# A hybrid encoder step in fp32: which groups of the two SwiGLU parts run as plain products and which as block products

## The chip, the cores and the metric

The kernel runs on one core of a Trainium2 chip, as one launch. The core has TensorE (PE, with its weight loads PEld), VectorE (DVE), ScalarE (ACT), GpSimd (POOL) and SyncE (SP), which issues the DMAs here. The metric is device time of one execution in microseconds: the median of three runs of the kernel before is 2302.98 us (2301.21 to 2305.12). Beside it stands one profiled execution.

## The reference

One layer of a streaming encoder on 1024 prompt tokens and 32 sample tokens, width 1024, all in fp32. Three sub-layers follow each other: a SwiGLU of inner width 2816, a pair of attention mixers side by side, and a second SwiGLU. Each is normalised before and after, and modulated by a vector `c` (one for the prompt, one for the sample):

```python
mod = jax.nn.silu(c) @ w_mod + b_mod
sh1, sc1, g1, sh2, sc2, g2, sh3, sc3, g3 = jnp.split(mod, N_MOD, axis=-1)
h = adaln_in(x, gains[0], sh1, sc1)
x = x + FFN_RES * g1[:, None] * rmsnorm(swiglu(h, w1_gate, w1_up, w1_down), gains[1])
...  # mixers with sh2, sc2, g2
h = adaln_in(x, gains[4], sh3, sc3)
x = x + FFN_RES * g3[:, None] * rmsnorm(swiglu(h, w2_gate, w2_up, w2_down), gains[5])
```

`swiglu(h)` is `(silu(h @ w_gate) * (h @ w_up)) @ w_down`. `w_mod` is 1024 x 9216, 36 MB of the weights.

## The kernel before, in words

**Layout and precision.** Activations lie with the width on partitions and tokens along the free axis. The 1056 tokens form three blocks: block 0 and block 1 with 384 tokens each, block 2 with 288 (256 of the prompt, 32 of the sample). A product of fp32 accuracy is made of three matmuls: each operand is split into a rounded part and a rest (ACT casts the first, `pair_of`; DVE or POOL subtracts for the second), and high x high, high x low and low x high are added up in PSUM (`product`).

**Two SwiGLU parts.** `ffn` is called twice, with the keys `h1` (first sub-layer) and `h3` (last). The inner width 2816 is cut into 11 groups of 256. A group has three stages: gate, up (`Mat`, weights of 1024 x 256, cut into four pieces A11 to A22 of 512 x 128) and down (`Rows`, 256 rows of `w_down`). A list of rounds says which group is done for which blocks; a stage is one round's gate, up or down, and the down stage of a round is queued behind the gate stage of the next. Each stage loads, casts and splits its own weights; the loads of the next stage start beside the present one.

**Plain and block products.** `plain` does one block: for each half f of the group's 256 columns two products of 12 matmuls (four k-tiles of 128 times three). Two blocks of 384 tokens then cost eight products a stage. `strassen` treats the pair (block 0, block 1) as one 2 x 2 block matrix product and needs seven: weight sums S1 to S4 on POOL (`ws`), token sums T1 to T4 made once for a part by `combos` (`z`, `t`), and ten additions a group on DVE that put the results together (tiles `sl` and `ut` from `gu` and `ge`). Block 2 stays plain inside it.

**Rounds before.** First part (`h1`): group 0 plain for the blocks as their norms come, groups 1 to 7 by block products with block 2 beside, groups 8 to 10 by block products for blocks 0 and 1 and then for block 2 alone. Last part (`h3`): group 0 plain for blocks 0 and 1, group 1 by block products, then groups 0 and 1 for block 2, then groups 2 to 10 by block products with block 2 beside.

**Work beside.** Generators in a list (`side`) do the other work in pieces: norms (`between`), `combos`, the rest of the modulation (`mod_all`), and the bias rows of the mixers (`bias_rows`). `step(n)` draws n pieces from the first of the list; `need` draws until one is done. Only the first 2048 columns of the modulation are made by matmuls at the start. The other 7168 columns go 384 at a time through `mod_aside`: four loads of 384 KB (`wma`), multiplied and accumulated for the prompt on DVE (`macc`, L247 and L249) and for the sample on ACT and POOL (`wmn`, `macc`, L250 to L255), then summed over partitions by small matmuls (`pms`) and turned into coefficients (`modT`, `acoef`, `gcoef`). Its buffers come from a pool of five that the weight sums, token sums and squares share. `per_group` is called with the group number after a round's up stage, and for round 0, whose up stage is done inside its gate stage, after the gate stage; for group 0 of the first part it is `mod_rest`, which starts the modulation and the bias rows.

**Order.** A scheduler sets each engine's order when the program is built; an engine then works through its queue in that order, and SP's queue of loads too. PSUM has two double banks for the down products and the pairs of block products (`p2`), and three single ones (`p1`). `r`, `w`, `ux`, `g`, `s` are the buffer counts of raw weights, split weights, extra activations, gated products and temporaries in a part.

## Time and profile before

| What | Value |
|---|---|
| median of three runs | 2302.98 us |
| profiled execution | 2300.64 us |
| its span, first to last instruction | 2298.9 us |
| mean granted TensorE clock | 0.966 |
| PE busy | 2140.8 us, 93% |
| DVE busy | 1449.5 us, 63% |
| ACT busy | 939.0 us, 41% |
| POOL busy | 810.0 us, 35% |
| moved by DMA | 186.10 MB, mean 81 GB/s |

The profile names engines, lines and tiles: `L249 DVE ... macc<-wma,csil,macc` is the accumulation of line 249 that writes `macc` from the loaded weights. The first SwiGLU runs from 42 to 894 us, the mixers follow, and the second SwiGLU starts at 1481 us. A matmul's own time overlaps the next one's, so a stage's time is read from the number of matmuls and the busy time of the stretch, and not from the mean of one. An engine's idle time is given with what ended it; idle time of an engine that nothing waits for costs nothing.

### The profile page before, as it was taken

The numbers are of one execution on the slowest core, as the hardware profiler recorded it, in microseconds if no ns is written. First come the engines' busy times: TensorE is split into PE (matmuls) and PEld (weight loads), VectorE is DVE, ScalarE is ACT, GpSimd is POOL, SyncE is SP. The second block draws the span as 40 slices with busy tenths as digits, with TensorE's granted clock in tenths as the row PEclk, the third lists the DMA queues.
The fourth block names the chain that finished last, engine by engine and source line by source line (L and its number), as shares of the span: only waits on it lengthen the run. The fifth ranks groups of instructions, "written<-read, shape, count | busy, mean of one in ns | idle before, by whom it ended". The sixth has DMA issues, their size and how long they took to land.

```text
span 2298.9 us, 35045 instructions
## 1 busy us (share of the span) xinstructions
PE 2140.8 (93%) x13644; PEld 2023.3 (88%) x13644; DVE 1449.5 (63%) x2722; ACT 939.0 (41%) x1990; POOL 810.0 (35%) x742
## 2 busy tenths in 40 slices
PE   7899999999999998999999899958999999999998
PEld 4888998999889997989888578858999999999997
DVE  5858667767775587667644775675644454444548
ACT  4454333433333344467644674434432223232225
POOL 2366555645554312200100322335133323332321
PEclk8999999999999998999999899979999999999999
DMA  8133323322342254110201211322311111111123
GB/s 322 59 94 113 92 78 92 117 80 89 95 129 72 65 187 144 54 48 25 66 14 39 80 37 47 134 61 66 111 56 56 46 46 56 56 38 54 38 65 115
DMA packets 150841, 186.10 MB, mean 81 GB/s; under 512 B 7980, under 2 KB 134356, under 8 KB 149524
## 3 DMA queue, kind: packets, MB, share of 16 engines
q1 hardware_dynamic: 150676, 183.87, 25.8%
q8 instruction: 107, 1.75, 0.3%
q14 instruction: 58, 0.48, 0.1%
HBM read 164.12 MB, written 22.86 MB: 81 GB/s over the span
## 4 chain that ended last, share of the span: by engine, by line
PE 54%; DVE 7%; POOL 4%; DMA 3%; ACT 2%; issue 2%; DVEq 0%; SPq 0%; POOLq 0%; ACTq 0%
PE gu L605 6%; PE ge L605 6%; PE dn L804 4%; PE dn L803 4%; PE dn L805 4%; PE g L605 4%; PE po L989 3%; POOL ws L570 2%; PE S L1028 2%; PE pq L349 2%; PE pq L351 2%; PE pq L350 2%; PE gate L605 2%; DMA raw<-in_w_up_dram 2%; PE pp L1052 1%
## 5 line engine op out<-in xcount | busy, mean ns | idle before, releaser
L547 DVE TENSOR_TENSOR w<-raw,w 128x512 fp32r<-128x512 f32 x298 | 257.2, 871 | 237.6 <-ACT w L546 229.2
L547 POOL TENSOR_TENSOR w<-ws,w 128x512 fp32r<-128x512 f32 x160 | 220.9, 1390 | 426.7 <-ACT w L546 426.7
L803 PE MATMUL dn<-gg,w 128*128 128x384 f32 (+1 forms) x1008 | 332.3, 330 | 16.8 <-DVE facc L810 10.7
L546 ACT ACTIVATE w<-raw 128x512 fp32r<-128x512 f32 x298 | 183.8, 627 | 370.1 <-PE gu L605 133.6
L804 PE MATMUL dn<-gg,w 128*128 128x384 f32 (+1 forms) x1008 | 326.6, 324 | 0.3 <-DVE gg L706 0.3
L805 PE MATMUL dn<-gg,w 128*128 128x384 f32 (+1 forms) x1008 | 326.1, 324 | 0.0
L810 DVE TENSOR_TENSOR facc<-dn,facc 128x768 f32<-128x768 f32 (+1 forms) x240 | 212.9, 887 | 179.6 <-PE dn L805 178.1
L605 PE MATMUL gu<-t,w 128*128 128x384 f32 x1440 | 265.4, 336 | 5.8 <-ACT w L546 3.6
L605 PEld LDWEIGHTS gu<-t,w 128*128 128x128 f32 x1440 | 249.1, 188 | 7.4 <-ACT w L546 3.9
L605 PE MATMUL g<-h_hi,w 128*128 128x288 f32 x1024 | 222.8, 295 | 1.5 <-DVE facc L810 1.5
L803 PEld LDWEIGHTS dn<-gg,w 128*128 128x128 f32 x1008 | 190.8, 189 | 24.4 <-DVE facc L810 14.9
L804 PEld LDWEIGHTS dn<-gg,w 128*128 128x128 f32 x1008 | 190.8, 189 | 0.6 <-DVE gg L706 0.6
L805 PEld LDWEIGHTS dn<-gg,w 128*128 128x128 f32 x1008 | 190.5, 189 | 0.0
L570 POOL TENSOR_TENSOR ws<-raw 128x512 f32<-128x512 f32 x80 | 118.5, 1482 | 194.9 <-DMA raw<-in_w_gate_dram 95.9
L605 PE MATMUL ge<-h,w 128*128 128x384 f32 x960 | 184.0, 335 | 0.1
L605 PEld LDWEIGHTS g<-h_hi,w 128*128 128x128 f32 x1024 | 172.0, 189 | 1.7 <-DVE facc L810 1.7
L546 ACT ACTIVATE w<-ws 128x512 fp32r<-128x512 f32 x160 | 98.6, 628 | 174.7 <-PE g L605 78.4
L605 PEld LDWEIGHTS ge<-h,w 128*128 128x128 f32 x960 | 166.4, 188 | 1.1 <-DVE w L547 0.7
L605 PE MATMUL g<-h_lo,w 128*128 128x288 f32 x512 | 151.4, 296 | 0.0
L249 DVE SCALAR_TENSOR_TENSOR macc<-wma,csil,macc 128x384 f32<-128x384 f32 (+1 forms) x133 | 123.6, 929 | 30.5 <-DMA wma<-in_w_mod_dram 29.0
L250 ACT ACTIVATE wmn<-wma,csil 128x384 f32<-128x384 f32 (+1 forms) x152 | 84.7, 602 | 117.7 <-DMA wma<-in_w_mod_dram 97.9
L605 PE MATMUL ge<-t,w 128*128 128x384 f32 x480 | 107.2, 362 | 23.1 <-ACT w L546 19.1
(298 smaller groups left out, 4625.5 us busy)
## 6 DMA issues: line engine op xcount, KB each, us to landing
raw<-in_w_gate_dram SPq DMA_DIRECT2D x54, 512.0 KB, 4.2
raw<-in_w_up_dram SPq DMA_DIRECT2D x54, 512.0 KB, 4.2
raw<-in_w_down_dram SPq DMA_DIRECT2D x54, 512.0 KB, 3.6
wma<-in_w_mod_dram SPq DMA_DIRECT2D x72, 384.0 KB, 3.3
raw<-in_w_in_dram SPq DMA_DIRECT2D x18, 512.0 KB, 4.5
raw<-in_w_out_dram SPq DMA_DIRECT2D x13, 512.0 KB, 4.3
wm<-in_w_mod_dram SPq DMA_DIRECT2D x8, 768.0 KB, 8.9
xr<-xs SPq DMA_DIRECT2D x16, 384.0 KB, 3.5
```

The source lines that it names most:

```text
L249: ve.scalar_tensor_tensor(acc[0], r[:, kk], csil[:, k, 0:1], acc[0], op0=OP.mult, op1=OP.add)
L250: ae.activation(n[:, kk], r[:, kk], AF.Copy, scale=csil[:, k, 1:2])
L349: te.matmul(ps, w[:, 0, k], hi, start=start, stop=False)
L546: ae.activation(w[:, 0], src, AF.Copy)
L547: (by or ve).tensor_tensor(w[:, 1], src, w[:, 0], op=OP.subtract)
L570: (ge if name in SUMS_POOL else ve).tensor_tensor(a[name], x, y, op=op)
L605: te.matmul(ps, w[a][:, k, :], x[b][k], start=first and k == 0 and q == 0, stop=last and k == n - 1 and q == 2, skip_group_check=True)
L803: te.matmul(ps[:, s, :w], h[:, k % 4, :], g[:, 0, :w], start=q == 0, stop=False)
L804: te.matmul(ps[:, s, :w], h[:, k % 4, :], g[:, 1, :w], start=False, stop=False)
L805: te.matmul(ps[:, s, :w], l[:, k % 4, :], g[:, 0, :w], start=False, stop=q == 1)
L810: ve.tensor_tensor(o, ps[:, :, :w], o, op=OP.add)
L989: te.matmul(po[64 * h:64 * h + 64, :n], vsl(j, h, kn), PT(h, j, kn), start=j == 0, stop=j == nt - 1)
```

## The change

It does five things.

- First part: groups 0 to 4 are plain (`PLAIN = 5`), groups 5 to 7 by block products with block 2 beside, groups 8 to 10 as before. `plain` takes several blocks of one stage, and draws five side pieces after every two products of a block, where round 0 drew ten and the block products one after each product; block products now draw two in both parts. `combos` is started at group 4's gate stage, ahead of all other side work, instead of at block 1 of round 0.
- Last part: groups 0 and 1 go plain for block 0, then for block 1, then for block 2 (`LEAD = 2`), and groups 2 to 10 by block products. Block 2's norm is started ahead of `combos`. The shared buffer `wu` for the first up stage is used in the first part alone.
- `combos` makes T3, T1 and T2 for both halves first and T4 last, and computes T4 from the finished T2.
- In rounds with one block, the low parts of A12, A22 and of the second half of the down weights are subtracted on POOL (`aside`, `shared`).
- The test ahead of `per_group` changes from "up stage, or gate stage of round 0" to "up stage, or round 0 of the first part", which holds for round 0's gate stage and for its down stage.

```diff
-ROUNDS = {"h1": (0, 3), "h3": (2, 0)}
+LEAD = 2
+LAST = 3
+PLAIN = 5
+STEPS = {"h1": (5, 5), "h3": (6, 6)}
...
-FFN2 = {"ux": 3, "r": 5, "w": 4, "g": 6, "s": 9}
+FFN2 = {"ux": 3, "r": 4, "w": 5, "g": 6, "s": 9}
...
+            self.aside = ("A12", "A22") if shared else ()
...
-                                          by=ge if name[0] == "S" else ve)
+                                          by=ge if name[0] == "S" or name in self.aside else ve)
...
-                self.w[q, hf] = pair_of(self.raw[q][:, 4 * hf:4 * hf + 4])
+                self.w[q, hf] = pair_of(self.raw[q][:, 4 * hf:4 * hf + 4], by=ge if self.shared and q else ve)
...
     def rounds(key):
...
+        both, n = (0, 1, 2), NF // 2
+        if key == "h3":
+            return [(g, (tb,)) for tb in both for g in range(LEAD)] + [(g, both) for g in range(LEAD, n)]
+        return [(g, both) for g in range(n - LAST)] + [(g, (0, 1)) for g in range(n - LAST, n)] + \
+            [(g, (2,)) for g in range(n - LAST, n)]
...
-        pace = PACE if key == "h1" else 2
+        pace = 2
+        fast = {r for r, (g, t) in enumerate(plan) if len(t) == 3 and (key == "h3" or g >= PLAIN) or len(t) == 2}
...
-            held = [stages.pop()] if r > 1 else []
+            held = [stages.pop()] if r else []
...
+                for tb in tbs:
+                    w = TB[tb][1]
                     ps = p1("gate" if what == "g" else "up")
...
+                    for d in range(2):
+                        product(ps[:, :w], w_[d], half(tb, d), d == 0, d == 1)
...
-                step((FAST if r == 0 else 3) if d else 2 * (r > 0))
+                    step(STEPS[key][len(tbs) > 1 or r == 0])
...
         if key == "h3":
+            begin((key, 2), between(F2[2], 2, 1, H3))
             begin((key, "T"), combos(H, T, tags))
-            begin((key, 2), between(F2[2], 2, 1, H3))
...
-                    if tb == 1 and key == "h1":
-                        begin((key, "T"), combos(H, T, tags))
...
+                if what == "g" and (key, gi) == ("h1", PLAIN - 1):
+                    begin((key, "T"), combos(H, T, tags), first=True)
+                plain(r, what, m, blocks, lambda n: nexts(n, 2 * len(blocks) - 1))
-            if what == "u" or r == 0 and what == "g":
+            if what == "u" or (key, r) == ("h1", 0):
                 if 2 in blocks:
                     per_group(gi)
```

The built program has 152 loads `wma` where it had 76. SP's queue just after the first part's x has been stored, before (`raw` are weights of a stage, `wma` the modulation's; x3 is three of the kind in a row):

```order
L586 DMA raw<-in_w_down_dram 128x1024 x2
L557 DMA raw<-in_w_gate_dram 128x4x256 x2
L557 DMA raw<-in_w_up_dram 128x4x256 x2
L241 DMA wma<-in_w_mod_dram 128x2x384 x7
L557 DMA raw<-in_w_gate_dram 128x4x256 x2
L241 DMA wma<-in_w_mod_dram 128x2x384 x3
```

and now:

```order
L244 DMA wma<-in_w_mod_dram 128x2x384 x9
L561 DMA raw<-in_w_gate_dram 128x4x256
L244 DMA wma<-in_w_mod_dram 128x2x384
L561 DMA raw<-in_w_gate_dram 128x4x256
L244 DMA wma<-in_w_mod_dram 128x2x384 x13
L590 DMA raw<-in_w_down_dram 128x1024 x2
L244 DMA wma<-in_w_mod_dram 128x2x384 x5
```

More modulation loads now stand between two loads of weights.

DVE's queue in group 2 of the first part, just ahead of the group's first accumulation of down products (`facc`), before:

```order
L249 SCALAR_TENSOR_TENSOR macc<-wma,csil,macc 128x384
L547 TENSOR_TENSOR w<-raw,w 128x512
L223 TENSOR_TENSOR modT<-modT,cst 128x2
L223 TENSOR_TENSOR modT<-modT,cst 128x2x2
L249 SCALAR_TENSOR_TENSOR macc<-wma,csil,macc 128x384
L227 SCALAR_TENSOR_TENSOR acoef<-modT,cst 128x2x2
L751 TENSOR_TENSOR sl<-gu,sl 128x384
L249 SCALAR_TENSOR_TENSOR macc<-wma,csil,macc 128x384 x2
L547 TENSOR_TENSOR w<-raw,w 128x512
L810 TENSOR_TENSOR facc<-dn,facc 128x768
```

and now:

```order
L252 SCALAR_TENSOR_TENSOR macc<-wma,csil,macc 128x384 x6
L250 TENSOR_SCALAR macc<-wma,csil 128x384
L252 SCALAR_TENSOR_TENSOR macc<-wma,csil,macc 128x384 x3
L267 COPY modT<-pms 128x2x3
L252 SCALAR_TENSOR_TENSOR macc<-wma,csil,macc 128x384
L226 TENSOR_TENSOR modT<-modT,cst 128x2x3
L252 SCALAR_TENSOR_TENSOR macc<-wma,csil,macc 128x384
L230 SCALAR_TENSOR_TENSOR acoef<-modT,cst 128x2x3
L550 TENSOR_TENSOR w<-raw,w 128x512
L252 SCALAR_TENSOR_TENSOR macc<-wma,csil,macc 128x384
L550 TENSOR_TENSOR w<-raw,w 128x512
```

Sixteen operations of the modulation (`macc`, `modT`, `acoef`) stand there now where seven stood, and the block additions (`sl<-gu`) are gone.

PE's queue at the start of the last part, from the second piece of the first gate stage on, before (`pr` spreads a norm's factor, `h` is the normalised block, `wu` the shared up weights):

```order
L605 MATMUL gate<-h,w 128x384 x13
L429 MATMUL pr<-ident,ry 128x128 x3
L605 MATMUL up<-h,wu 128x384 x4
L605 MATMUL gate<-h,w 128x384 x18
L605 MATMUL up<-h,wu 128x384 x32
L605 MATMUL up<-h,w 128x384 x12
```

and now:

```order
L609 MATMUL gate<-h,w 128x384 x13
L609 MATMUL up<-h,w 128x384 x22
L432 MATMUL pr<-ident,ry 128x128 x3
L609 MATMUL up<-h,w 128x384 x26
L609 MATMUL gate<-h,w 128x384 x48
```

Block 0's up stage and the gate stage of the next group for block 0 now follow where block 1 of the same group stood.

More of the change, by code (lines that the diff above doesn't have):

```diff
@@ L596, in split @@
             ae.activation(t[:, 0], self.raw[q], AF.Copy)
-            ve.tensor_tensor(t[:, 1], self.raw[q], t[:, 0], op=OP.subtract)
+            (ge if self.shared and q else ve).tensor_tensor(t[:, 1], self.raw[q], t[:, 0], op=OP.subtract)
             for h in range(2):
@@ new lines, in combos, with cut, whole @@
+        tags = dict(tags)
+        def cut(name, s, v):
+            o = t[name]
+            ae.activation(o[:, 0, s, :], v, AF.Copy)
+            ve.tensor_tensor(o[:, 1, s, :], v, o[:, 0, s, :], op=OP.subtract)
+        def whole(x, s, e):
+            z = h_tile([128, 2, 384], "z")
+            e.tensor_tensor(z, x[:, 0, s, :].bitcast(F32), x[:, 1, s, :].bitcast(F32), op=OP.add)
+            return z
+        for name in ("T3", "T1", "T2"):
+            t[name] = u(tags[name], name.lower())
@@ L631, in combos @@
+        steps = (slice(0, 2), slice(2, 4))
+        for s in steps:
+            z11 = whole(H[1][2][1], s, ge)
+            z10 = whole(H[1][2][0], s, ve)
+            z00 = whole(H[0][2][0], s, ge)
             yield
-            cut("T3", z[1, 1])
-            ve.tensor_tensor(z[1, 0], z[1, 0], z[0, 0], op=OP.subtract)
+            ve.tensor_tensor(z11, z11, z10, op=OP.subtract)
             yield
-            cut("T1", z[1, 0])
-            ve.tensor_tensor(z[0, 0], z[0, 0], z[1, 1], op=OP.add)
+            cut("T3", s, z11)
+            ve.tensor_tensor(z10, z10, z00, op=OP.subtract)
@@ L637, in combos @@
             yield
-            cut("T2", z[0, 0])
-            ve.tensor_tensor(z[0, 1], z[0, 1], z[0, 0], op=OP.subtract)
+            cut("T1", s, z10)
+            ve.tensor_tensor(z00, z00, z11, op=OP.add)
             yield
-            cut("T4", z[0, 1])
+            cut("T2", s, z00)
+            yield
+        t["T4"] = u(tags["T4"], "t4")
+        for s in steps:
+            z01 = whole(H[0][2][1], s, ve)
+            z2 = whole(t["T2"], s, ge)
+            yield
+            ve.tensor_tensor(z01, z01, z2, op=OP.subtract)
+            yield
+            cut("T4", s, z01)
@@ L646, in rounds @@
     def rounds(key):
-        lead, lag = ROUNDS[key]
-        both, n, out = (0, 1, 2), NF // 2, []
-        if lead:
-            out += [(g, (0, 1)) for g in range(lead)] + [(g, (2,)) for g in range(lead)]
-        out += [(g, both) for g in range(lead, n - lag)]
-        out += [(g, (0, 1)) for g in range(n - lag, n)] + [(g, (2,)) for g in range(n - lag, n)]
-        return out
+        both, n = (0, 1, 2), NF // 2
[3 more added lines that the diff above has]
+            [(g, (2,)) for g in range(n - LAST, n)]
     STRASSEN = [("A11", "B11", "a", 2), ("A12", "B21", "a", 2), ("S2", "T2", "b", 0), ("S1", "T1", "d", 0),
@@ L673, in load @@
             gi, blocks = plan[r]
+            alone = len(blocks) == 1
             if what == "d":
-                loaded[r, what] = Rows(wd, gi, "ux" if key == "h1" and blocks == (2,) else "w")
+                loaded[r, what] = Rows(wd, gi, "ux" if key == "h1" and alone else "w", alone)
             else:
-                loaded[r, what] = Mat((wg, wu)[what == "u"], gi)
+                loaded[r, what] = Mat((wg, wu)[what == "u"], gi, alone)
         def ready(i):
@@ L688, in ready @@
                 m.split(1, 0)
-            elif r and plan[r][1] != (2,):
+            elif r in fast:
                 m.of("S4")
+                m.split("A11")
             else:
                 m.split("A11")
+                m.split("A12")
         def made(r, what, f, tb, src):
```

70 lines of the change are left out of this document (24 added, 46 removed).

## The prediction

> **What bounds the kernel now.** I read the page's busy line and its slices first, then tables of busy time by stretch, then the waits of PE in the two places that the change touches.
>
> ```profile
> PE 2140.8 (93%) x13644; PEld 2023.3 (88%) x13644; DVE 1449.5 (63%) x2722; ACT 939.0 (41%) x1990; POOL 810.0 (35%) x742
> ```
>
> PE is busy for 93% of the span, so what can be gained is what it idles; the mean hides where that is. By stretch (columns: length, then busy us of PE, PEld, DVE, ACT and POOL with their instructions, granted clock, DMA share, GB/s), the first row is the first SwiGLU from the first down products to group 7, the second the start of the second SwiGLU, the third one undisturbed group of it:
>
> ```profile
> 100.00:701.00 601.00, 555.41 (x3388) 540.55 (x3387) 423.56 (x603) 230.49 (x436) 346.84 (x265) 0.97 0.32 97
> 1481.00:1664.00 183.00, 146.22 (x849) 141.86 (x850) 125.26 (x216) 77.61 (x142) 63.13 (x44) 0.89 0.28 88
> 1765.00:1831.00 66.00, 65.34 (x410) 64.90 (x409) 32.54 (x46) 18.29 (x35) 22.37 (x16) 1.00 0.16 49
> ```
>
> An undisturbed group of block products costs 66 us, with 32.5 of DVE. The same groups beside the modulation run slower (74 to 79 us each below), because DVE has 53 to 56 us to do in them and PE waits for splits and accumulations that stand behind the modulation's:
>
> ```profile
> 324.00:402.00 78.00, 72.63 (x449) 70.98 (x448) 55.74 (x77) 29.80 (x57) 49.56 (x39) 0.98 0.32 97
> 402.00:476.00 74.00, 69.79 (x433) 68.59 (x432) 52.65 (x74) 27.12 (x52) 37.56 (x31) 0.98 0.32 97
> 476.00:555.00 79.00, 73.32 (x443) 71.63 (x443) 53.06 (x73) 29.15 (x57) 48.42 (x38) 0.96 0.31 91
> ```
>
> PE's waits in the first stretch, and then in the second (us in total, times, longest):
>
> ```profile
> PE ge L605 <- ACT w L546: 16.4, 8, 3.5
> PE dn L803 <- DVE facc L810: 10.3, 12, 1.7
> ...
> PE up L605 <- ACT wu L546: 19.6, 1, 19.6
> PE gate L605 <- DVE w L547: 4.5, 1, 4.5
> ```
>
> So there are two stores of idle PE time: 601 - 555.4 = 46 us beside the modulation, in small pieces, and 183 - 146.2 = 37 us at the start of the second SwiGLU, more than half of it one wait of 19.6 us for split weights.
>
> **The change, part by part.** PE first. Four groups of the first part and one of the second go from seven block products to eight: per group two stages with 12 matmuls more. The undisturbed group gives 65.34 us / 410 = 0.16 us a matmul. First part: 4 x 24 x 0.16 = 15.4 us; second part: 24 x 0.16 = 3.8 us. Both lie on PE.
>
> What is not in the change's few words decides the first part: the test that starts the modulation and the bias rows after round 0 no longer asks for the gate stage, and round 0's down stage passes it too. The modulation and bias generators are started twice, so the program issues 152 loads of modulation weights where it had 76, and computes all coefficients twice with the same values. What one pass costs in the first stretch, on DVE, POOL and ACT:
>
> ```profile
> L249 DVE SCALAR_TENSOR_TENSOR macc<-wma,csil,macc 128x384 f32<-128x384 f32 (+1 forms) x133 | 123.6, 929 | 30.5 <-DMA wma<-in_w_mod_dram 29.0
> L547 DVE TENSOR_TENSOR w<-raw,w 128x512 fp32r<-128x512 f32 x94 | 92.5, 988 | 65.4 <-ACT w L546 57.6 <-DMA raw<-in_w_down_dram 4.6 <-POOL macc L255 2.9
> L751 DVE TENSOR_TENSOR sl<-gu,sl 128x384 f32<-128x384 f32 x32 | 17.6, 549 | 4.4 <-PE gu L605 4.2
> L704 DVE TENSOR_TENSOR sl<-sl,ut 128x384 f32<-128x384 f32 x21 | 19.8, 945 | 0.1
> L247 DVE TENSOR_SCALAR macc<-wma,csil 128x384 f32<-128x384 f32 (+1 forms) x19 | 10.0, 528 | 0.3 <-DMA wma<-in_w_mod_dram 0.3
> L223 DVE TENSOR_TENSOR modT<-modT,cst 128x6 f32<-128x6 f32 (+2 forms) x23 | 9.1, 408 | 0.4
> L547 POOL TENSOR_TENSOR w<-ws,w 128x512 fp32r<-128x512 f32 x63 | 89.2, 1427 | 97.3 <-ACT w L546 97.3
> L255 POOL TENSOR_TENSOR macc<-macc,wmn 128x384 f32<-128x384 f32 (+1 forms) x57 | 67.6, 1187 | 2.5
> L253 POOL TENSOR_TENSOR wmn<-wmn 128x384 f32<-128x384 f32 (+1 forms) x57 | 66.8, 1172 | 100.9 <-ACT wmn L250 99.4 <-issue 1.4
> L253 POOL TENSOR_TENSOR macc<-wmn 128x384 f32<-128x384 f32 (+1 forms) x19 | 22.8, 1200 | 22.1 <-ACT wmn L250 22.0
> L250 ACT ACTIVATE wmn<-wma,csil 128x384 f32<-128x384 f32 (+1 forms) x152 | 84.7, 602 | 117.7 <-DMA wma<-in_w_mod_dram 97.9
> ```
>
> DVE: the second pass adds 123.6 + 10.0 + 9.1 = 143 us. Plain groups drop the additions that put block products together, ten a group at 0.55 us, so 4 x 5.5 = 22 us, and three products a group with the gate's SiLU read PSUM there, at the additions' 0.55 us for L704's 0.95: 12 x 0.4 = 5 us less. Net +116 us: 424 becomes 540 us. POOL: +157 us for the pass (67.6 + 66.8 + 22.8), less 16 weight sums and their splits in each of four groups, at about 1.43 us (the split's row): 64 x 1.43 = 92 us; net +65 us, 347 becomes 412. ACT: +85 us less 32 splits at 0.6 us; 230 becomes 295 us, which bounds nothing. DMA: 76 x 384 KB more at a share of 0.32; not a bound in bytes, but these loads stand in SP's one queue ahead of the weights, and a load waits there until one of five shared buffers is free. DVE already sat 29 us before accumulations that waited for such loads.
>
> Where it falls: the plain groups take five side steps after every two products of a block where the block groups took one after each product, so the first pass is over by about group 3. DVE's order has 100 modulation accumulations before the end of group 1 and 52 in group 2, against 40 and 18 before. The second pass then lies in groups 4 to 8, at two steps a product. In both halves DVE has more to do than before, and every group's accumulations (facc) stand in DVE's queue behind that work, with two PSUM buffers for PE to run ahead: PE cannot leave DVE behind.
>
> How long does the stretch become? Below it cannot come under PE's own 555.4 + 15.4 = 571 us, and some of the short chain waits stay: 590, which is 11 us less than now. Above: all of DVE's 116 us on the path, 717 us. Between them I go by how full DVE gets where PE waits for it, in pieces of 50 us:
>
> ```profile
> 50.00:100.00 50.00, 43.12 (x259) 41.67 (x257) 41.23 (x90) 24.56 (x56) 15.62 (x14) 0.90 0.24 87
> 850.00:900.00 50.00, 41.81 (x293) 41.06 (x292) 43.42 (x85) 19.91 (x33) 9.93 (x8) 0.91 0.50 156
> 1500.00:1550.00 50.00, 26.48 (x129) 25.59 (x130) 41.56 (x60) 20.30 (x33) 19.49 (x9) 0.73 0.20 57
> ```
>
> 82 to 87%, and PE is at 53 to 86% there. 540 us at 83% are 651 us: **+50 us**. Taking 87% it would be 621 (+20), at 80% 675 (+74).
>
> Tail of the first part (groups 8 to 10, block 2 apart): twelve splits go from DVE to POOL, a last piece of the second pass comes in, and DVE has 140 us to do in 199:
>
> ```profile
> 701.00:900.00 199.00, 188.27 (x1169) 184.40 (x1168) 140.22 (x225) 76.14 (x130) 62.46 (x46) 0.98 0.36 111
> ```
>
> **+4 us** (0 to +8): there is room, but the last second-pass coefficients have to be done before the first part ends.
>
> Second part, from the timeline (start, length, engine and line; the first two rows are DVE's, the next ACT's, the last PE's):
>
> ```profile
> 1461.99 5.60 DVE L478 SCALAR_TENSOR_TENSOR h<-n,modT,h 128x384 fp32r<-128x384 f32 x6
> ...
> 1503.64 7.63 DVE L478 SCALAR_TENSOR_TENSOR h<-n,modT,h 128x384 fp32r<-128x384 f32 x6
> ...
> 1517.57 0.84 ACT L627 ACTIVATE t<-z 128x768 fp32r<-128x768 f32 x1 [0.90 <-DVE z L636]
> 1518.32 1.65 ACT L546 ACTIVATE wu<-raw 128x512 fp32r<-128x512 f32 x3
> ...
> 1518.99 2.05 PE L605 MATMUL up<-h,wu 128*128 128x384 f32 x4 [19.59 <-ACT wu L546]
> ```
>
> Block 0 is normalised by 1468 us and block 1 by 1511; the first gate starts at 1481. PE then stands until 1519, since the up weights' cast on ACT (wu) is queued behind the casts of the combinations T, and these wait for DVE. Afterwards PE has two groups of block 0, two of block 1 and two of block 2 before it needs T: block 0 alone gives 2 x 144 matmuls, 46 us, to 1527, when block 1 has been there for 16 us. What is late next is DVE: 125 us of work in the stretch today, about 13 us less afterwards, since ten block additions go (5.5 us) and twelve of 48 splits (0.6 to 0.9 us each); though each group's weights are split three times, half of the splits are POOL's, 36 at 1.43 us = 51 us on top of its 63. Six matrices more to load, 1 MB each, add 6 MB to 88 GB/s over 183 us (16 MB), which the DMA share of 0.28 carries. Floor: 146 + 4 = 150 us of PE, less some 5 for the clock (0.89 granted in the stretch today, 1.00 undisturbed). No gain at all would be 183. I take the floor plus the 4.5 us wait of the first gate, which stays, and 6 us for the new splits' chain over two engines: 161 us (DVE then has 112 us to do in them, 70%), **-22 us** (-38 to +4). One raw buffer fewer is costed at 0: a stage needs two and the next two more, four in all, and the undisturbed stage of 20 us covers two loads of 4.2 us (page, DMA issues); without that cover it is a few us a group.
>
> Sum against the profiled execution: 2298.9 span + 50 + 4 - 22 = 2331 us, plus the 1.7 us that lie around the span (2300.64 in all): **2333 us**. That execution stands 2.3 us under the median of the runs.
>
> **The rivals.** (1) The second pass disappears into DVE's idle time. DVE idles 177 of 601 us today, and modulation is never urgent; if the order puts it only where DVE would have waited, the stretch keeps to PE's 571 us plus some waits, 590 (-11), and the second part gives its best, -30: 2300.6 - 11 - 30 = 2260 us. For it: in an undisturbed group DVE is at 49%. Against it: it would need DVE at 540 / 590 = 92% for 600 us, and the three fullest pieces above have 82 to 87%; from about 90% on this case holds. (2) The second part gives nothing back, because POOL's splits and DVE's norms take the place of the wait: 2300.6 + 50 + 4 + 4 = 2359 us. For it: the wait of 4.5 us for DVE's split is there today, and DVE has 83% in 1500 to 1550. Against it: the 19.6 us are one wait of a kind that the new order does not have. (3) DVE and POOL shut each other out. DVE's operations come in two lengths (min, median and max in ns):
>
> ```profile
> L249 DVE SCALAR_TENSOR_TENSOR macc<-wma,csil,macc x133: 483/621/1727, 120.5 to 668.3; 128x384 f32<-128x384 f32 x126, 128x256 f32<-128x256 f32 x7
> L547 DVE TENSOR_TENSOR w<-raw,w x94: 616/708/1822, 101.9 to 700.9; 128x512 fp32r<-128x512 f32 x94
> ```
>
> The longest accumulation is the median plus 1.1 us, one POOL addition (1.19). If work on SBUF of the two engines never runs at once, the first stretch holds 133 x 0.62 + 94 x 0.71 = 149 us of DVE and POOL's 347: 496 of 601. The change adds 83 and 65: 644 us. With 5% unfilled that is 678, +77: 2300.6 + 77 + 4 - 22 = 2360 us. For it: those lengths. Against it: POOL's 347 us hold waits of its own, so the sum may be some tens too high; it decides over the forecast if the two fill over 95% of the time. The Trainium skill, page "SBUF — State Buffer", section "SBUF: two separate sides", states this rule: a DVE instruction with two SBUF inputs and a GpSimd instruction that reads SBUF take one port pair by an exclusive lock for the whole instruction. The lengths above agree with it. That the change does less than its diff says can be excluded: the built order has each modulation load twice.
>
> **How the numbers follow.** Forecast 0.56, rival (1) 0.25, rival (2) 0.10, rival (3) 0.09. The forecast's own range is 2300 to 2385: 20 us less to 24 us more in the first stretch, 16 either way in the second part. The range over all cases leaves out the lower half of rival (1) and the upper end of (3): 2266 to 2388. Within 0.2%, or 4.6 us of the median, is what a measurement of this kernel can tell from no change. Faster by more: rival (1), 0.25; within: 0.06, the forecast's low end; slower: the rest, 0.50 + 0.10 + 0.09 = 0.69.
>
> **What will show it.** Right: 152 modulation loads and 266 accumulations on L249's successor; DVE above 80% from 100 us to the end of group 7, which comes 30 to 70 us later than at 701; groups 2 and 3 the longest; more waits of PE for split weights and accumulations; no wait near 20 us at the start of the second SwiGLU, and the stretch from its first gate to the first three-block Strassen group at 150 to 170 us. Wrong: group 7 ends by 700 us with DVE at 90% or above (rival 1), the second stretch stays above 178 us (rival 2), or group 7 ends after 770 us with DVE's mean accumulation well above 0.93 us (rival 3). A first part shorter by 40 us would mean that plain groups remove a wait that I have not seen.

## The result and the profile after

The changed kernel takes 2371.2 us (median of four runs, 2369.16 to 2373.79), the kernel before beside it 2303.31 us: a ratio of 1.0296 with an interval of 1.0278 to 1.0314, 68 us slower. The forecast was 2333 us in a range of 2266 to 2388: the direction and the range were right, the size was less than half of it.

The page's busy line of the changed kernel:

```profile
PE 2197.4 (93%) x13988; PEld 2083.5 (88%) x13988; DVE 1572.6 (66%) x2891; ACT 1010.4 (43%) x2118; POOL 928.3 (39%) x850
```

All engines have more to do: PE 57 us, DVE 123, POOL 118. The 344 more matmuls on PE are 120 of the extra products and 224 small ones (`pms`) that sum the modulation over partitions, now twice:

```profile
L265 PE MATMUL pms<-ones,macc 128*128 128x1 f32 x448 | 58.2, 248 | 24.5 <-DVE macc L252 24.3
```

(columns: matmuls, busy us, mean ns, and the idle time ahead of them). Before there were 224, at 27.6 us, with 2.3 us of idle ahead.

Where the time went is read from points that all kernels pass. The first three are ends of accumulations (`facc`): of group 7, of the rounds for blocks 0 and 1 alone, and of the whole first part. Then come the last part's first gate, its first product of a three-block group, and the end. All are times in us of the profiled execution; `once` is the first experiment below.

| Point | before | after | `once` |
|---|---|---|---|
| group 7 done | 700.8 | 749.8 | 688.1 |
| groups 8 to 10 done for blocks 0 and 1 | 830.4 | 896.2 | 817.7 |
| first part done | 900.2 | 972.1 | 893.0 |
| first gate of the last part | 1481.4 | 1555.5 | 1471.2 |
| first three-block group there | 1665.6 | 1736.4 | 1649.7 |
| end | 2298.9 | 2367.4 | 2281.3 |

From before to after the lengths between these points change by +49, +17, +6, +2, -3 and -2 us: together 68.5. The first part has become 72 us longer, and the last part gives back 5.6.

The tables by stretch, as in the prediction (length, busy us of PE, PEld, DVE, ACT and POOL with instructions, clock, DMA share, GB/s): the same first 601 us, the stretch to the new end of group 7, and the start of the second SwiGLU.

```profile
100.00:701.00 601.00, 553.64 (x3431) 542.28 (x3430) 485.04 (x699) 262.69 (x492) 358.25 (x296) 0.97 0.43 131
100.00:750.00 650.00, 599.35 (x3687) 586.76 (x3687) 527.02 (x753) 283.65 (x530) 392.25 (x323) 0.97 0.43 131
...
1555.00:1736.00 181.00, 148.16 (x880) 145.86 (x881) 124.72 (x199) 87.45 (x159) 90.52 (x64) 0.90 0.39 122
```

DVE is busy for 527 of 650 us, 81%. PE idles 51 us there, and its waits in this stretch have changed their kind (total, times, longest):

```profile
PE pms L265 <- DVE macc L252: 23.9, 9, 4.5
PE dn L821 <- DVE facc L828: 14.4, 18, 3.0
PE gu L609 <- DVE sl L769: 5.4, 1, 5.4
```

The wait of 16.4 us for weights cast on ACT no longer shows. In its place PE waits for the modulation itself, 23.9 us in nine waits: the small sums stand in PE's queue among the products, behind accumulations that DVE has not done yet.

At the start of the second SwiGLU the wait of 19.6 us for `wu` is gone, and the stretch is nearly as long as it was, because of other waits:

```profile
PE dn L821 <- ACT facc L826: 18.6, 2, 15.3
PE gate L609 <- DVE w L550: 5.1, 2, 4.4
PE pr L432 <- DVE ry L365: 4.4, 1, 4.4
```

### The profile page after: what moved, and what is told of

It is laid out like the page before. It is cut to its first block, busy times and chain, and to the rows that moved or that the text cites. A ratio compares the mean times of both kernels' runs of the same rounds, so it can differ in the third digit from the quotient of the medians.

```text
span 2367.4 us, 36544 instructions
## 1 busy us (share of the span) xinstructions
PE 2197.4 (93%) x13988; PEld 2083.5 (88%) x13988; DVE 1572.6 (66%) x2891; ACT 1010.4 (43%) x2118; POOL 928.3 (39%) x850
## 4 chain that ended last, share of the span: by engine, by line
PE 63%; DVE 19%; DMA 7%; POOL 4%; issue 3%; ACT 2%; SPq 0%; DVEq 0%; POOLq 0%; ACTq 0%
PE gu L609 7%; PE ge L609 6%; DVE macc L252 5%; PE dn L821 5%; PE dn L822 5%; PE dn L823 5%; PE up L609 5%; PE gate L609 4%; PE g L609 4%; DMA wma<-in_w_mod_dram 4%; PE po L1003 2%; PE S L1042 2%; PE pq L352 2%; DVE w L550 2%; PE pq L354 2%
## 5 line engine op out<-in xcount | busy, mean ns | idle before, releaser
L821 PE MATMUL dn<-gg,w 128*128 128x384 f32 (+1 forms) x1008 | 335.0, 333 | 37.0 <-ACT facc L826 18.6
L550 POOL TENSOR_TENSOR w<-ws,w 128x512 fp32r<-128x512 f32 x120 | 169.0, 1415 | 287.3 <-ACT w L549 268.7
L252 DVE SCALAR_TENSOR_TENSOR macc<-wma,csil,macc 128x384 f32<-128x384 f32 (+1 forms) x266 | 245.2, 922 | 47.2 <-DMA wma<-in_w_mod_dram 43.4
L253 ACT ACTIVATE wmn<-wma,csil 128x384 f32<-128x384 f32 (+1 forms) x304 | 168.2, 604 | 177.4 <-DMA wma<-in_w_mod_dram 135.2
L821 PEld LDWEIGHTS dn<-gg,w 128*128 128x128 f32 x1008 | 192.4, 191 | 44.7 <-DVE facc L828 19.6
L609 PE MATMUL gu<-t,w 128*128 128x384 f32 x1080 | 207.0, 343 | 9.0 <-DVE sl L769 7.7
L256 POOL TENSOR_TENSOR wmn<-wmn 128x384 f32<-128x384 f32 (+1 forms) x114 | 126.8, 1112 | 199.0 <-ACT wmn L253 172.7
L609 PEld LDWEIGHTS gu<-t,w 128*128 128x128 f32 x1080 | 192.8, 194 | 11.0 <-DVE sl L769 8.3
L609 PE MATMUL g<-h_hi,w 128*128 128x288 f32 x768 | 164.7, 295 | 1.3 <-DVE facc L828 1.3
L258 POOL TENSOR_TENSOR macc<-macc,wmn 128x384 f32<-128x384 f32 (+1 forms) x114 | 135.4, 1188 | 7.1
L609 PE MATMUL ge<-h,w 128*128 128x384 f32 x720 | 137.9, 335 | 0.0
L609 PE MATMUL gate<-h,w 128*128 128x384 f32 x672 | 125.0, 341 | 8.5 <-DVE w L550 5.1
```

The lines of the kernel that those rows point to most:

```text
L252: ve.scalar_tensor_tensor(acc[0], r[:, kk], csil[:, k, 0:1], acc[0], op0=OP.mult, op1=OP.add)
L253: ae.activation(n[:, kk], r[:, kk], AF.Copy, scale=csil[:, k, 1:2])
L256: ge.tensor_tensor(to, n[:, 0], n[:, 1], op=OP.add)
L258: ge.tensor_tensor(acc[1], acc[1], n[:, 0], op=OP.add)
L550: (by or ve).tensor_tensor(w[:, 1], src, w[:, 0], op=OP.subtract)
L609: te.matmul(ps, w[a][:, k, :], x[b][k], start=first and k == 0 and q == 0, stop=last and k == n - 1 and q == 2, skip_group_check=True)
```

## The experiments

Two questions were open: what the second pass of the modulation costs, and through which engine; and what holds the last part's gain back. Two theories stood against each other on the first: that DVE's time is full (the forecast's), and that DVE and POOL shut each other out (rival 3).

**The modulation once.** The test asks for the gate stage again; all else is the changed kernel.

```diff
-            if what == "u" or (key, r) == ("h1", 0):
+            if what == "u" or (key, r, what) == ("h1", 0, "g"):
```

> The changed kernel with the modulation and the bias rows started once, after round 0's gate stage alone. Theory (the second pass is the first part's whole loss): the mixers start at 880 to 900 us instead of 973, DVE below 75% beside the modulation, and the total is 2285 to 2300 us. Rival (the plain groups and their order cost the first part its time, and the second pass runs in DVE's idle time): the mixers start at 950 us or later and the total stays above 2345 us.

Measured: 2279.05 us, ratio 0.9895 [0.9878, 0.9913]. Without the second pass the change is a gain of 24 us; with it a loss of 68. So the second start, a pass of the modulation and a second set of bias rows, costs 92 us in the medians, 79 of them in the first part (893.0 against 972.1). The gain is larger than was expected. The plain groups themselves bring the first part 7 us by this mark, and 1 us by the mixers' first matmul (895.2 and 894.4): they lose where the first pass is packed into groups 1 and 2 (these are done at 358 us, against 324 before), and win afterwards, when groups 4 to 6 go undisturbed in 66 to 67 us each. The last part keeps its wait of 15.3 us.

**The pass twice in the kernel before.** The reverse: the old kernel, with the new test's effect alone.

```diff
-            if what == "u" or r == 0 and what == "g":
+            if what == "u" or r == 0 and (what == "g" or key == "h1"):
```

> The kernel before with the modulation and the bias rows started twice and nothing else changed. Theory (a second pass costs wherever DVE and POOL are shared): the total is 2360 to 2400 us, 60 to 100 us over the kernel before, and all of it lies ahead of the mixers. Rival (a second pass only costs because the change packs it into fewer groups): 2303 to 2330 us.

Measured: 2479.48 us, ratio 1.0769 [1.0746, 1.0791], +175 us: nearly twice what it costs in the changed kernel, and far over what was expected. Group 7 ends at 702 us, 2 us later than without the second pass. At one side piece per product the first pass lasts almost to there, and most of the second finds no products left to run beside: it is drained ahead of the mixers, and PE stands. Waits of PE from 700 to 1056 us, and the busy table of 880 to 1000:

```profile
PE pms L262 <- DVE macc L249: 84.0, 13, 7.5
```

```profile
880.00:1000.00 120.00, 36.22 (x175) 35.21 (x174) 115.13 (x141) 55.93 (x101) 98.35 (x85) 0.54 0.56 168
```

So the change's quicker drawing of side pieces did take in most of the second pass: in the changed kernel 40 of its 133 accumulations are done by the end of group 4, and 82 more in groups 5 to 7. The doubling is dear in both forms, but more so in the old.

**Parts of the second pass.** Five kernels are the changed one with a second pass that is cut down (`mod_aside` stays for the first, whose coefficients are used). All leave out work that is computed twice; the pieces and their number stay.

```diff
     def mod_all(first):
+        passes[0] += 1
+        again = passes[0] > 1
...
-            yield from mod_aside(c0, min(3, 72 - c0))
+            yield from (mod_part if again else mod_aside)(c0, min(3, 72 - c0))
```

`mod_part` has the four loads of a piece alone; or these with DVE's multiplications and accumulations; or these with ACT's multiplications and POOL's additions; or these with both engines' work and without the sums on PE and what follows them; or nothing but the small matmuls on PE, made from constants, and one copy. All five also start the bias rows a second time, which `once` does not.

> The changed kernel, whose second pass only loads its weights and computes nothing with them (the coefficients of the first pass are used). Theory (the second pass costs by the work on DVE and POOL): most of the loss goes, and the total comes within 15 us of the kernel that starts the modulation once. Rival (the loads in SP's queue and the five shared buffers make the weights late): the total stays above 2340 us.

> The changed kernel, whose second pass loads its weights and does DVE's accumulation, without the sample's part on ACT and POOL and without the sums on PE. The loads alone put the mixers at 908 us (one pass: 894), all but the sums at 957. Theory (DVE's own time is the price, as the prediction's sum had it): mixers at 940 to 957 us, total 2332 to 2348. Rival (DVE and POOL shut each other out, so each alone costs little and the two together much): mixers at 910 to 925 us, total 2303 to 2318.

> The changed kernel, whose second pass loads its weights and does the sample's part on ACT and POOL, without DVE's accumulation and without the sums on PE. Theory (DVE's own time is the price): mixers within 8 us of the loads' 908, total 2300 to 2312. Rival (DVE and POOL shut each other out): 910 to 925 us alone, and the two parts' prices over the loads add up to less than half of the 50 us that both cost together. A third (POOL is the bound, since its additions take 1.2 us and are in front of the weight sums): mixers at 935 us or later.

> The changed kernel, whose second pass loads, multiplies and accumulates as it did, but leaves out its sums over partitions on PE (the small matmuls pms) and the coefficients behind them. The changed kernel started the mixers at 973 us, the one with a single pass at 894. Theory (PE's own part of a pass, 29 us of small matmuls and their waits for DVE's accumulation, is over half of the price): mixers at 925 to 940 us, total 2318 to 2338. Rival (the price is DVE and POOL being full, as the prediction had it): mixers at 960 us or later, total 2355 or more.

> The changed kernel, whose second pass does nothing but the small matmuls on PE, from a constant instead of the accumulated products, and one copy of each result. Theory (they cost their busy time on PE, since PE bounds the first part): 25 to 35 us over the kernel with one pass, total 2304 to 2316. Rival (they fall into PE's gaps): under 10 us over it, total below 2290.

Measured, with the first matmul of the mixers (`pv`) as the mark of the first part's length; it stands at 894.4 us without a second pass and at 973.4 with the whole of it:

| Second pass has | time, us | ratio | `pv` at | over none |
|---|---|---|---|---|
| loads | 2306.14 | 1.0011 [1.0001, 1.0022] | 907.6 | 13.2 |
| loads, DVE's part | 2309.4 | 1.0030 [1.0017, 1.0043] | 916.3 | 21.9 |
| loads, ACT's and POOL's part | 2316.13 | 1.0056 [1.0037, 1.0075] | 920.8 | 26.4 |
| loads, DVE's, ACT's and POOL's part | 2348.24 | 1.0197 [1.0181, 1.0214] | 957.3 | 62.9 |
| PE's small matmuls alone | 2305.9 | 1.0017 [1.0004, 1.0030] | 915.8 | 21.4 |
| all | 2371.2 | 1.0296 [1.0278, 1.0314] | 973.4 | 79.0 |

Over the loads, DVE's part alone adds 8.7 us, ACT's and POOL's 13.2, and both 49.7: more than twice the sum of the two. These marks are of one execution each; by the medians the three are 3, 10 and 42 us. The sums on PE add the last 16.1. The second bias rows come behind group 7's end in all five kernels; from there to the end of the first part the kernel with loads alone takes 1.1 us more than `once`, and the one with PE's sums alone 2.5, so they are a small part of these prices. Several expectations were missed: the loads cost less than their rival and more than their theory had, and both parts together stay short of the 960 us that would have spoken for a full DVE and POOL. A theory that I held between the first runs and these, that PE's sums are over half of the price, fell with the fourth row. The forecast's own, that DVE's time alone is the price, fell with the second. In the 260 us from 430 to 690, first with DVE's part alone, then with both parts:

```profile
430.00:690.00 260.00, 244.52 (x1482) 238.44 (x1481) 198.05 (x288) 66.82 (x123) 77.44 (x56) 0.99 0.45 138
```

```profile
430.00:690.00 260.00, 228.00 (x1325) 222.37 (x1323) 197.26 (x245) 111.62 (x211) 175.98 (x139) 0.95 0.37 114
```

DVE is busy for 198 and 197 us, and gets 288 instructions done in the one and 245 in the other. The accumulations show it, in the same two kernels and the same stretch (count, busy us, mean ns):

```profile
L291 DVE SCALAR_TENSOR_TENSOR macc<-wma,csil,macc 128x384 f32<-128x384 f32 x105 | 77.9, 743 | 7.5 <-DMA wma<-in_w_mod_dram 6.0
L572 DVE TENSOR_TENSOR w<-raw,w 128x512 fp32r<-128x512 f32 x44 | 39.4, 897 | 25.6 <-ACT w L571 25.6
```

```profile
L292 DVE SCALAR_TENSOR_TENSOR macc<-wma,csil,macc 128x384 f32<-128x384 f32 x86 | 79.3, 922 | 30.2 <-DMA wma<-in_w_mod_dram 29.0
L579 DVE TENSOR_TENSOR w<-raw,w 128x512 fp32r<-128x512 f32 x37 | 38.8, 1056 | 17.4 <-ACT w L578 16.3 <-issue 0.9
```

743 against 922 ns for one shape: the busy time grows by waiting inside the instruction. What it waits for can be counted in the trace. Of the 105 accumulations 80 meet no POOL instruction, and of the 86 only 22; all of these last 0.60 to 0.62 us. The others last up to 1.71 and 1.66. DVE's operations with an input in PSUM do not lengthen here. Two operations in the same two kernels, a subtraction with both inputs in SBUF (`gg`) and an addition that reads PSUM (`gu`), min, median and max in ns:

```profile
L746 DVE TENSOR_TENSOR gg<-sl,gg x22: 443/550/1544, 430.2 to 659.1; 128x384 fp32r<-128x384 f32 x14, 128x288 fp32r<-128x288 f32 x8
L791 DVE TENSOR_TENSOR sl<-gu,sl x16: 543/553/558, 449.8 to 671.3; 128x384 f32<-128x384 f32 x16
```

```profile
L753 DVE TENSOR_TENSOR gg<-sl,gg x21: 453/806/1609, 429.9 to 689.4; 128x384 fp32r<-128x384 f32 x13, 128x288 fp32r<-128x288 f32 x8
L798 DVE TENSOR_TENSOR sl<-gu,sl x12: 541/546/559, 451.1 to 632.3; 128x384 f32<-128x384 f32 x12
```

POOL's additions lengthen too, when DVE's part joins (the kernel with ACT's and POOL's part, then with both):

```profile
L294 POOL TENSOR_TENSOR macc<-macc,wmn 128x384 f32<-128x384 f32 x43 | 48.2, 1121 | 2.1
```

```profile
L298 POOL TENSOR_TENSOR macc<-macc,wmn 128x384 f32<-128x384 f32 x38 | 46.1, 1213 | 1.7
```

Rival 3's sum puts the three kernels in order. Accumulations at 0.62 and splits at 0.71 us, its two medians, plus POOL's busy time, are for DVE's part alone 65 + 31 + 77 = 173 of 260 us, 67%; with both parts 53 + 26 + 176 = 255, 98%. With ACT's and POOL's part alone DVE has the 44 splits and no accumulations (31 us), and POOL this row's 180.7:

```profile
430.00:690.00 260.00, 245.78 (x1482) 241.65 (x1481) 133.94 (x169) 127.71 (x243) 180.74 (x153) 0.97 0.46 139
```

212 us, 82%. The sum doesn't show that the time is full, because POOL's busy time holds its own waits and is so counted twice in part. By the trace, POOL or a DVE operation with two inputs in SBUF is at work for 170, 201 and 220 of the 260 us (65, 77 and 85%, in the order of the table), and both at once for 43, 53 and 99. What is shown is that the two slow each other and that together they cost far more than singly. A second way in which they meet isn't separated from this: loads, products and weight sums share five buffers, and with both parts DVE idles 31.6 us ahead of its multiplications and accumulations for a load, where with its own part alone it idles 9.9.

**The last part's new wait.** In the changed kernel, rows of ACT's timeline and then of PE's (start, length, engine and line, idle before):

```profile
1626.10 3.18 ACT L479 ACTIVATE h_hi<-n,modT 128x256 fp32r<-128x256 f32 x10 [8.97 <-DVE n L455]
...
1639.29 0.84 ACT L624 ACTIVATE t<-z 128x768 fp32r<-128x768 f32 x1 [6.94 <-DVE z L640]
1640.04 1.50 ACT L826 ACTIVATE facc<-dn 128x768 f32<-128x768 f32 x2
```

```profile
1597.21 0.33 PE L823 MATMUL dn<-gg,w 128*128 128x384 f32 x1
...
1612.80 3.28 PE L609 MATMUL gate<-h,w 128*128 128x384 f32 x18
...
1640.88 0.69 PE L821 MATMUL dn<-gg,w 128*128 128x384 f32 x1 [15.34 <-ACT facc L826]
```

The down products of block 0, group 0, have filled both PSUM banks by 1597 us. The next ones wait for a bank, which the first copies of block 0's down result (`facc`) free. These copies stand in ACT's queue behind the normalisation of block 2 and the first cast of a token sum (`t`). PE does no matmul of a product from 1616 to 1641 us. Three explanations: ACT's queue as such, the order in which the work was asked for, or POOL's splits (rival 2's). The first was tested by making these copies on DVE:

```diff
-            if owns[tb]:
+            if owns[tb] and key == "h3":
+                ve.tensor_copy(o, ps[:, :, :w])
+            elif owns[tb]:
```

> The changed kernel; in the last part the first group's down products are copied out of PSUM by DVE instead of ACT. Theory (the 25 us without main matmuls after 1616 us come from ACT's copy that is queued behind the token combinations' casts): the stall shrinks to under 12 us and the total is 2350 to 2362 us. Rival (PE would then wait for block 2's norm or for DVE in the same place, whose own queue holds the combinations too): 2366 to 2376 us.

Measured: 2371.44 us, ratio 1.0295 [1.0273, 1.0318]: nothing gained. The wait has moved with the copies:

```profile
PE dn L821 <- DVE facc L826: 19.0, 2, 16.3
```

So it isn't ACT's queue as such; on DVE too the copies stand behind block 2's norm and the first operations of the token sums. In the program, block 0's result and two of the four token sums (T3, the first made, and T2) take their buffers from one pool (`ux`), in the order in which they are asked for. The next kernel starts the token sums later: `once`, with `combos` begun at the first gate stage of block 1 and not ahead of the part.

```diff
-            begin((key, "T"), combos(H, T, tags))
...
+            if (key, r, what) == ("h3", LEAD, "g"):
+                begin((key, "T"), combos(H, T, tags))
```

> One pass of the modulation, and in the last part the token combinations are started with block 1's first round instead of ahead of the part. Theory (the first copies of block 0's down products are put behind the combinations' first cast in the order, because their buffer comes from the same pool and is asked for after T3's): no stall of 15 us before the down products of round 0, the stretch from the first gate to the first three-block product 155 to 168 us instead of 178, total 2262 to 2272. Rival (block 2's norm holds the copies up): the stall stays above 10 us and the total is within 5 us of 2279.

Measured: 2260.43 us, ratio 0.9809 [0.9787, 0.9831], 18.6 us under `once` and the fastest of all. The stretch falls from 178.5 to 160.6 us, where the prediction had 161, and no long wait is left. POOL has the same splits to do in this kernel, so they weren't the wait either:

```profile
1473.00:1634.00 161.00, 148.20 (x882) 145.21 (x883) 129.49 (x199) 86.54 (x160) 90.70 (x64) 0.96 0.44 143
```

```profile
PE dn L822 <- DVE gg L724: 5.3, 2, 4.8
PE gate L609 <- DVE w L550: 5.1, 2, 4.5
```

**POOL's splits in the first part's tail.** In the rounds for block 2 alone, fifteen splits went from DVE to POOL: twelve of A12 and A22 and three of the down weights. `once` with the sharing kept to the last part:

```diff
+            shared = alone and key == "h3"
...
-                loaded[r, what] = Rows(wd, gi, "ux" if key == "h1" and alone else "w", alone)
+                loaded[r, what] = Rows(wd, gi, "ux" if key == "h1" and alone else "w", shared)
...
-                loaded[r, what] = Mat((wg, wu)[what == "u"], gi, alone)
+                loaded[r, what] = Mat((wg, wu)[what == "u"], gi, shared)
```

> One pass of the modulation, and in the first part's rounds of block 2 alone the low parts of A12, A22 and of the second down half are subtracted on DVE again; the last part keeps POOL. With one pass the last three groups took 124 us (770 to 894) where the kernel before took 112. Theory (POOL's slow splits in those rounds make up that difference): mixers at 880 to 886 us, total 2266 to 2273. Rival (the difference comes from elsewhere, as the second start of the bias rows or the larger stock of side work did before): mixers within 4 us of 894.

Measured: 2274.7 us, ratio 0.9877 [0.9860, 0.9894]. The rounds for block 2 in the kernel before, in `once` and with DVE's splits again:

```profile
830.00:900.00 70.00, 59.84 (x423) 58.23 (x421) 62.17 (x113) 31.87 (x53) 17.14 (x12) 0.94 0.51 162
```

```profile
818.00:893.00 75.00, 61.37 (x414) 58.69 (x413) 67.54 (x100) 31.37 (x52) 38.70 (x25) 0.90 0.47 151
```

```profile
812.00:882.00 70.00, 59.55 (x421) 57.95 (x419) 62.40 (x114) 32.14 (x52) 17.13 (x12) 0.93 0.50 162
```

In `once` these rounds have thirteen operations fewer on DVE, and DVE is busy 5 us longer with the rest: the splits on POOL cost these rounds 5 us. The last part's first gate comes 9.4 us sooner, but its stretch is 4.8 us longer (183.3): the wait for the late copies is still there, 15.7 us. Half of a gain ahead of a wait has become wait.

**All together.** Both edits in one kernel, and the same with three side pieces after every two products of the first part in place of five.

```diff
-STEPS = {"h1": (5, 5), "h3": (6, 6)}
+STEPS = {"h1": (3, 3), "h3": (6, 6)}
```

> One pass of the modulation, the token combinations started with block 1's first round, and block 2's low parts of the first part on DVE. Each alone came out at 2279, 2260 (with one pass) and 2275 us (with one pass). If their gains lie in different places they add up: 2279 - 19 - 4 = 2256 us, range 2250 to 2262. If the first part's gain only moves a wait into the start of the mixers or of the last part: 2260 to 2266.

> The same, and the plain groups of the first part draw three side pieces after two products instead of five, so that the one pass lies in groups 1 to 4 (72, 106, 128 and 152 accumulations done at their ends) and not in groups 1 and 2 (100 and 152). Theory (groups 1 and 2 are slow, 263 and 358 us at their ends against 248 and 324 in the kernel before, because a pass is packed into them, and DVE has idle time in groups 3 and 4): the mixers start 10 to 25 us earlier, total 2232 to 2248. Rival (a pass costs the same wherever it lies): within 5 us of the kernel with five pieces.

Measured: 2265.68 us, ratio 0.9837 [0.9821, 0.9854], and 2272.63 us, 0.9865 [0.9845, 0.9884]. The gains don't add. The first part is shorter with both edits, as with the tail's alone, and the last part's first gate comes at 1464.7 us, 8.7 us before `once_tlate`'s; but the stretch behind it takes 167.4 us, 6.8 more. With three pieces, groups 1 and 2 end at 255 and 341 us (263 and 358 in `once`), and group 7 at 685, where `three` also has it. The pass costs as much spread over four groups as packed into two.

## Why the prediction was right or wrong

**To group 7's end: +50 forecast, +49 measured.** DVE has 527 us in 650, 81%, for a forecast of 540 at 83%. But it is a net of two things the sum had not separated: plain groups with one pass gain 13 us here (700.8 to 688.1), and the second pass costs 62 (to 749.8). That the two agree to 1 us is luck. And the reason given, that DVE's time is full, is only half right. DVE's part alone, with DVE as busy, costs the first part 8.7 us over the loads. What costs the time is DVE and POOL together, the mechanism that I had as rival 3 with a chance of 0.09. Its own sum for this stretch, by its medians and the two rows here (busy us, mean ns of 100 to 750 us), with POOL's 392 us from the table above:

```profile
L252 DVE SCALAR_TENSOR_TENSOR macc<-wma,csil,macc 128x384 f32<-128x384 f32 (+1 forms) x255 | 234.2, 918 | 45.0 <-DMA wma<-in_w_mod_dram 41.3
L550 DVE TENSOR_TENSOR w<-raw,w 128x512 fp32r<-128x512 f32 x92 | 92.8, 1013 | 24.8 <-ACT w L549 24.7
```

255 x 0.62 + 92 x 0.71 + 392 = 615 of 650 us, 95%, where it was 83% before. The point from which I let it decide was 95%, and the stretch comes to it, though part of POOL's time is counted twice there, as above. Its own end of group 7, 778 us, was too late by 28, as its sentence on POOL's busy time, which holds waits of its own, allowed for. So the term was hit with a rate and not with a cause: 83% isn't the most that DVE shows, since in 880 to 1000 us of the old kernel with two passes it is busy at 96%, waits inside its instructions included.

**The tail: +4 forecast, +23 measured** (+17 and +6). This is the first step that failed. I took what is left of the second pass behind group 7's end to fit into the room there. It is little, 11 accumulations, the last at 776.6 us, and the bias rows behind them to 804; but the rounds of groups 8 to 10 for blocks 0 and 1 take 146 us where `once` and the kernel before have 130. The loss lies at their start. The first 40 us behind group 7, now and in `once`:

```profile
749.80:790.00 40.20, 34.50 (x175) 32.73 (x173) 33.24 (x55) 17.06 (x33) 32.77 (x26) 0.87 0.31 93
```

```profile
688.10:728.00 39.90, 39.65 (x228) 39.01 (x227) 23.87 (x33) 12.27 (x23) 16.56 (x12) 1.00 0.27 80
```

PE does 175 matmuls there where it does 228 in `once`: it idles 5.7 us instead of 0.3, and its granted clock is 0.87 instead of 1.00. The kernels with a cut second pass take 131 us for these rounds with the loads or PE's sums alone, 138 and 137 with DVE's or with ACT's and POOL's part, and 142 with both: it is again the work on DVE and POOL. The other 6 us are in `once` as well, and the experiment on the splits names them: the splits that I counted as twelve, and costed at nothing because DVE gave them up, are fifteen and cost 5 us. POOL takes 1.42 us on average for one of 128x512 in `once`, where DVE takes 0.71 in the kernel before.

**The second part: -22 forecast, -5.6 measured** (-3.3 in the stretch itself). The second step that failed, and with 16 us the other large part of the error. The stretch was sized right: 161 us appear in `once_tlate`. Its working was not: DVE has 129 us to do in them and not 112, and the 5 us that the floor was to lose to the clock are named but not in the sum. The wait that I removed had a successor that I did not look for. I asked what DVE does next, and not what frees the PSUM banks of block 0's first down products. This is rival 2's outcome (the stretch above 178 us) by a mechanism that rival 2 did not name: neither POOL's splits nor DVE's norms, but the place behind the token sums that the late copies got. That the late copies are queued behind the token sums, and that asking for these later removes the wait, is shown; that the pool's order is what holds them was read from the program, and not separated from the mere place of the casts in the queues.

**PE's sums were left out.** I priced a pass on DVE, POOL and ACT. It also has 224 small matmuls on PE, 27.6 us of busy time, in the row L262 of the profile before. They add 16 us as the last part and 21 alone, 18.9 of these by group 7's end. In the stretch to group 7 the error is hidden in the rate; the wait for them was not forecast at all, and is PE's largest there.

**Signs.** Right: 152 loads and 266 accumulations; DVE over 80%; group 7 within the 30 to 70 us; no wait of `wu`. Wrong: groups 2 and 3 were to be the longest; group 2 is (92.5 us), group 3 is the shortest of 2 to 7 (72.1). More waits for split weights and accumulations were expected; the first are fewer, the second 14.4 us instead of 10.3. The stretch of 150 to 170 us is 181. The upper end of the forecast's own range isn't what its terms give: 24 us more in the first stretch, 16 in the second part and 4 in the tail lead to 2377 and not to 2385.

**Rival 1** saw the second pass vanish in DVE's idle time, 2260 us. That is nearly the time of `once_tlate`, but for another reason: there the pass isn't made twice. With DVE's part alone it nearly holds: 8.7 us over the loads for what I had priced at 134 us of DVE, the multiplications and accumulations of the 143.

**What stays open.** The medians of the kernels with a cut second pass lie 5 to 14 us further above `once` than their first part explains (loads: 27.1 against 13.2). Single executions of one kernel lie up to 11 us apart (2310.2 to 2321.3 with ACT's and POOL's part), and the profiled one of `once`, from which its marks are read, is the slowest of its four (2283.08). From it to the profiled one with the loads alone it is 20.4 us, of which 3.3 are in the mixers and 4.3 at the start of the last part; why these stages differ was not tested.

## What to carry to other kernels

Price a piece of side work on every engine that it touches, the small matmuls on PE and the waits ahead of them too, and before reading how full one engine is, add DVE's operations with two SBUF inputs to POOL's time: here sums of 67 and 82% of the stretch went with losses of 9 and 13 us, and a sum of 98% with 50. When a wait is removed, follow the first instruction behind it to its operands and its output buffer, and ask who takes that buffer first. And a condition that is widened by a word is worth counting in the built program: here it made work double, and 92 us hung on it, more than on all that the change set out to move.

## What the runs showed of the hardware

DVE and POOL slow each other without either being full. Added singly to the same program their parts cost 8.7 and 13.2 us, together 49.7; one accumulation of 128x384 lasts 743 ns on average beside a quiet POOL and 922 beside a busy one, and 0.60 to 0.62 us whenever it meets no POOL instruction. DVE's additions that read PSUM stay at 0.54 to 0.56 us beside both. The Trainium skill, page "SBUF — State Buffer", section "SBUF: two separate sides", has the lock that would do this: an instruction of DVE with two SBUF inputs and one of GpSimd that reads SBUF hold it for their whole length, each against the other. The trace agrees with it in kind. It does not agree that nothing overlaps: in the drain of the old kernel with two passes (880 to 1000 us), the 84 accumulations and 12 multiplications of DVE and the 85 additions of POOL below would take 52 + 5 + 86 us one after the other, at the 0.62 us and 0.41 us that the two last without a POOL instruction beside them and at the 1.01 us that an addition lasts beside a quiet DVE, and they are done in 120. POOL's spans in the profile are rough, so the size of the overlap is too.

```profile
L249 DVE SCALAR_TENSOR_TENSOR macc<-wma,csil,macc 128x384 f32<-128x384 f32 (+1 forms) x84 | 86.1, 1025 | 3.4 <-DMA wma<-in_w_mod_dram 1.4
...
L253 POOL TENSOR_TENSOR wmn<-wmn 128x384 f32<-128x384 f32 (+1 forms) x37 | 43.5, 1176 | 23.6 <-ACT wmn L250 23.6
L255 POOL TENSOR_TENSOR macc<-macc,wmn 128x384 f32<-128x384 f32 x36 | 43.4, 1206 | 2.8
...
L253 POOL TENSOR_TENSOR macc<-wmn 128x384 f32<-128x384 f32 (+1 forms) x12 | 13.4, 1121 | 2.9 <-ACT wmn L250 2.9
L247 DVE TENSOR_SCALAR macc<-wma,csil 128x384 f32<-128x384 f32 (+1 forms) x12 | 12.4, 1037 | 0.4 <-DMA wma<-in_w_mod_dram 0.4
```

A matmul of one column is not cheap: 224 of them with their weight loads, for one pass, take 27.6 us of PE's busy time, and alone make group 7 end 18.9 us later. The loads of a pass, 29 MB more beside the weights, make the first part 13.2 us longer, although the DMA share with them is 0.45 in the middle of the first part:

```profile
430.00:690.00 260.00, 243.43 (x1484) 241.85 (x1484) 121.98 (x168) 67.00 (x124) 78.04 (x58) 0.98 0.45 143
```

The trace of the kernel with the loads alone shows where, from 430 to 690 us: POOL's weight sums, whose buffers come from the same five, wait for modulation loads to land, and PE waits for the splits of these sums.

```profile
POOL ws L592 <- DMA wma<-in_w_mod_dram: 58.8, 8, 14.2
```

```profile
PE gu L627 <- POOL w L568: 13.7, 3, 5.4
```

In `once` PE's waits of this second kind come to 1.8 us up to group 7's end. That more buffers would remove the cost was not tried.
